# Forms of the input made in place and in smaller steps, weight splits of one stretch at a higher priority, sums of weights behind their low parts, and a buffer moved by 32 bytes

## The chip, the core and the metric

The kernel runs on one core of a Trainium2 chip. The core has five engines with queues of their own: PE (TensorE, matmuls), DVE (VectorE), ACT (ScalarE), POOL (GpSimd) and SP (SyncE, which here only issues transfers). They share an on-chip memory of 128 partitions; matmuls add into a smaller memory, PSUM. The metric is the device time of one execution in microseconds (us), lower is better. Of the kernel before three runs are shown, of which the median counts.

## What is computed

One layer of a decoder on 256 rows of 2048 numbers, float32. Cut to the projections around the change:

```python
h = rms_norm(x, ln1_g[l])
proj = h @ w_in[l]
aq, ak, av, iq, ik, iw, rq, rk, rv, rg, ga, gb = jnp.split(proj, offsets, axis=-1)
o_attn = dsa_attention(...)                    # top-k of an indexer, 16 heads
y_ret = retention_chunkwise(rq, rk, rv, log_gamma)
o_ret = jax.nn.silu(rg) * group_norm_heads(y_ret, ...)
merged = jax.nn.sigmoid(ga) * (o_attn @ w_up_attn[l]) + jax.nn.sigmoid(gb) * (o_ret @ w_up_ret[l])
x = x + merged @ w_out[l]
x = x + jnp.square(jax.nn.relu(rms_norm(x, ln2_g[l]) @ w_ff1[l])) @ w_ff2[l]
```

The change touches the projections `ga` and `gb` (the gates, 2048 columns each) and what is made for them.

## The kernel before

**One product.** Every large product is made of three fp32r matmuls. A float32 number is split into a high part, rounded to fp32r, and a low part, the rest. `split` (L337) does this for 128x1024 weights at a time: ACT copies them to fp32r (`whi`, L350), and DVE subtracts that from the raw weights (`wlo`, L351). `products` (L397) then issues, for each 128x512 of weights and each activation, high times high (L401), high activation times low weight (L402) and low activation times high weight (L403). The weights are the moving operand, the activations are the stationary one. `whi` and `wlo` have three buffers each. Raw weights of 128x2048 float32 (1 MB) arrive by SP's queue into one of three places: a ring of four, a pair of buffers `rawb` in the pool `cx`, or the two halves of `rawc`. Loads are asked for up to eight items ahead of their use, splits two items ahead (`ahead`, L360).

**The woven stretch.** The four gate units GA0, GA1, GB0 and GB1 (1024 columns each) are made in seven products instead of eight half-size ones, as in Strassen's scheme. Four of the seven have a weight quarter plus another one, or a form of the input, a difference of two of its quarters, as a factor. A unit has 28 items Q0 to Q27 of 6 matmuls, four for each product. They are woven with 80 items of 12 matmuls of other projections: RV2 and RV3, UA0 to UA3, RQ0 and RQ1, RK0 and RK1, eight items each (RV2.0 is the first of RV2). The order is written by `gates` (L132): Q0, RV2.0, Q1, RV2.1, Q2, RV2.2, Q3, Q4, RV2.3, Q5, RV2.4, Q6, Q7 and so on. `strassen` (L640) makes an item Q; behind the last item of each product it copies the result out (ACT) or adds it into results that stand on chip (DVE, L657), and where a quarter of the result is finished, `gate` applies the sigmoid (ACT, L462) and sends it to memory (POOL). These results and copies are called `stg`.

**Sums of weights.** Quarter A plus B, B plus C, C plus A and D plus C are made by DVE at L343, on 128x2048 elements in place in the raw buffer of the first. The table `SUMS` (L119) says ahead of which item each is made; `split` issues it just before that item's high part.

**Forms of the input.** G5, G6, G3 and G7 are kept as high and low parts in `hx` (4 forms of 128x1024 each, twice). Before the first gate, between the blocks RV0 and RV1, two tiles `xr` are loaded with the transposed input (L738). They take the two `rawb` buffers, into which weights go afterwards. `h_forms` (L698) runs as a generator beside the matmuls of RV1, one step at a time, each step between two pieces of the block: ACT multiplies `xr` by the gains (L704, 16 instructions of 128x256, two steps of eight), then for each form DVE subtracts (L710, 128x1024, into a tile `tmp`), ACT copies the high part (L711) and DVE subtracts the low part (L712). `tmp` has the tag `big2` with a single buffer, and `rawc` follows in the same buffer; so no load into `rawc` can start before `tmp` is done with. RV2's weights, the first of the woven stretch to use `rawc`, come that way.

**What sets the order.** All code is written as one stream of instructions, and a scheduler orders each engine's part by priority, which follows the place in the stream, and by when operands are expected. On the chip each engine then works strictly in that order.

## Time and profile before

| What | Value |
|---|---|
| Time, median of 3 runs | 1642.29 us (1640.89 to 1643.23) |
| The profiled execution's own time | 1642.31 us |
| Its span, first to last instruction | 1640.5 us |
| Mean granted TensorE clock | 0.997 |
| Woven stretch | from about 272 us to 670 us |
| Load of `xr`, issue to landing | 6.4 us |

The profile takes its times from one execution. A row of the timeline has the start in us from the span's start, the duration in us, the engine, the line, the operation, out<-in with the tiles' names, the shape and a count of equal instructions in a row; in brackets the idle time before it and what ended that. Matmuls are pipelined: a row lasts about 0.39 us, and the next one starts after 0.23 us. In the table of windows each engine has its busy time and the number of its instructions in the stretch, and PEclk is the mean granted clock. A row of the tile view has minimum, median and maximum of the durations in ns and the first and last start in us. A wait row has total us, times and longest us.

### The profile page before, as it was taken

To read this page: it belongs to the slowest core of one execution; us is meant where nothing else is said; L and a number is where in the kernel's file an instruction comes from. 1 tells how busy PE (TensorE), PEld (TensorE's weight loads), DVE (VectorE), ACT (ScalarE), POOL (GpSimd) and SP (SyncE) were. 2 spreads that over 40 slices of the span, in tenths; PEclk is the share of its full clock that TensorE was granted. 3 is DMA by queue.
4 is the path that set the end of the run, shared out by engine and by line. 5 is a ranking of instruction groups with operands and counts; after the bars stand their busy time and mean duration, and the time that the engine had idled before them with its cause. 6 is when DMAs were issued, how large, how long until landed. Compare 5 with 4: busy or idle time off the path is not lost.

```text
span 1640.5 us, 19424 instructions
## 1 busy us (share of the span) xinstructions
PE 1622.0 (99%) x7366; PEld 1330.5 (81%) x7366; DVE 1268.3 (77%) x1307; ACT 1000.1 (61%) x1238; POOL 100.4 (6%) x141
## 2 busy tenths in 40 slices
PE   9999998999999999999999999999999999999998
PEld 8977886788878778888888878888888888888887
DVE  5577675878787898677665478898989898989874
ACT  7556566566565656544444576766767676767672
POOL 0000000000000000000110000000000000000000
PEclk9999999999999999999999999999999999999999
DMA  9634347465567645744777654767777777667583
GB/s 333 224 132 178 133 150 281 162 232 209 218 246 277 225 148 187 263 154 177 259 256 261 214 210 188 234 228 231 231 231 231 231 231 226 228 217 230 176 252 134
DMA packets 68206, 353.88 MB, mean 216 GB/s; under 512 B 7696, under 2 KB 14480, under 8 KB 31888
## 3 DMA queue, kind: packets, MB, share of 16 engines
q1 hardware_dynamic: 51616, 311.32, 51.3%
q0 software_dynamic: 13760, 35.14, 9.7%
q10 hardware_dynamic: 2736, 6.18, 1.0%
q8 instruction: 58, 0.95, 0.2%
q14 instruction: 36, 0.29, 0.0%
HBM read 325.34 MB, written 27.26 MB: 215 GB/s over the span
## 4 chain that ended last, share of the span: by engine, by line
PE 90%; DVE 5%; issue 2%; ACT 2%; DMA 1%; POOL 0%; DVEq 0%; SPq 0%; ACTq 0%; POOLq 0%
PE pm L402 14%; PE pm L403 14%; PE pm L401 13%; PE pq L402 8%; PE pq L403 8%; PE pq L401 8%; PE pf L401 7%; PE pf L403 7%; PE pf L402 7%; DVE wlo L351 2%; PE pt L430 1%; ACT whi L350 1%; PE pa L628 1%; PE pa L601 1%; DVE raw L343 1%
## 5 line engine op out<-in xcount | busy, mean ns | idle before, releaser
L351 DVE TENSOR_TENSOR wlo<-raw,whi 128x1024 fp32r<-128x1024 f32 (+2 forms) x528 | 626.9, 1199 | 243.0 <-ACT whi L350 236.9
L350 ACT ACTIVATE whi<-raw 128x1024 fp32r<-128x1024 f32 (+2 forms) x528 | 546.3, 1041 | 405.2 <-PE pm L403 270.7
L402 PE MATMUL pm<-wlo,act 128*128 128x512 f32 (+1 forms) x1056 | 409.7, 388 | 8.6 <-DVE wlo L351 8.6
L401 PE MATMUL pm<-whi,act 128*128 128x512 f32 (+1 forms) x1056 | 414.7, 397 | 1.8 <-ACT whi L350 1.8
L403 PE MATMUL pm<-whi,act 128*128 128x512 f32 (+1 forms) x1056 | 408.3, 387 | 0.0
L351 DVE TENSOR_TENSOR wlo<-rawc,whi 128x1024 fp32r<-128x1024 f32 x192 | 234.2, 1220 | 59.1 <-ACT whi L350 57.4
L350 ACT ACTIVATE whi<-rawc 128x1024 fp32r<-128x1024 f32 x192 | 203.4, 1059 | 102.8 <-PE pm L403 44.2
L402 PEld LDWEIGHTS pm<-wlo,act 128*128 128x128 f32 x1056 | 199.1, 189 | 53.0 <-DVE wlo L351 15.3
L401 PEld LDWEIGHTS pm<-whi,act 128*128 128x128 f32 x1056 | 198.6, 188 | 43.7 <-ACT whi L350 4.0
L403 PEld LDWEIGHTS pm<-whi,act 128*128 128x128 f32 x1056 | 199.0, 188 | 38.0
L343 DVE TENSOR_TENSOR raw<-raw,raw 128x2048 f32<-128x2048 f32 x88 | 201.1, 2285 | 0.8
L401 PE MATMUL pf<-whi,act 128*128 128x512 f32 x512 | 200.1, 391 | 0.0
L402 PE MATMUL pf<-wlo,act 128*128 128x512 f32 x512 | 199.4, 389 | 0.0
L403 PE MATMUL pf<-whi,act 128*128 128x512 f32 x512 | 199.4, 389 | 0.0
L401 PE MATMUL pq<-whi,xf 128*128 128x512 f32 x392 | 154.4, 394 | 0.0
L403 PE MATMUL pq<-whi,xf 128*128 128x512 f32 x392 | 152.8, 390 | 0.0
L402 PE MATMUL pq<-wlo,xf 128*128 128x512 f32 x392 | 152.6, 389 | 0.0
L401 PEld LDWEIGHTS pf<-whi,act 128*128 128x128 f32 x512 | 96.1, 188 | 20.1 <-ACT whi L350 0.4
L403 PEld LDWEIGHTS pf<-whi,act 128*128 128x128 f32 x512 | 96.1, 188 | 20.1
L402 PEld LDWEIGHTS pf<-wlo,act 128*128 128x128 f32 x512 | 96.2, 188 | 19.8
L403 PEld LDWEIGHTS pq<-whi,xf 128*128 128x128 f32 x392 | 73.6, 188 | 15.4
L402 PEld LDWEIGHTS pq<-wlo,xf 128*128 128x128 f32 x392 | 73.7, 188 | 14.7
(167 smaller groups left out, 1416.4 us busy)
## 6 DMA issues: line engine op xcount, KB each, us to landing
raw<-in_w_dram SPq DMA_DIRECT2D x180, 1024.0 KB, 5.8
rawc<-in_w_dram SPq DMA_DIRECT2D x96, 1024.0 KB, 5.8
sums<-ev POOLq DMA_DIRECT2D x56, 256.0 KB, 5.5
raw<-in_w_dram SPq DMA_DIRECT2D x8, 736.0 KB, 4.7
raw<-in_w_dram SPq DMA_DIRECT2D x7, 512.0 KB, 7.3
raw<-in_w_dram SPq DMA_DIRECT2D x8, 368.0 KB, 7.7
stg<-in_x_dram SPq DMA_DIRECT2D x8, 256.0 KB, 7.6
rv<-stg POOLq DMA_DIRECT2D x8, 256.0 KB, 4.3
```

What stands on the lines that cost most here:

```text
L343: nc.vector.tensor_tensor(one, one, two, op=ALU.add)
L350: nc.scalar.activation(a, src, AF.Copy)
L351: nc.vector.tensor_tensor(b, src, a.bitcast(F32), op=ALU.subtract)
L401: nc.tensor.matmul(d, h, hi, start=first, stop=False, skip_group_check=skip)
L402: nc.tensor.matmul(d, h, lo, start=False, stop=False, skip_group_check=skip)
L403: nc.tensor.matmul(d, l, hi, start=False, stop=last, skip_group_check=skip)
L430: nc.tensor.transpose(ps[:, c * P:(c + 1) * P], src[:, c * P:(c + 1) * P], ident)
L601: nc.tensor.matmul(ps[:, a * n:(a + 1) * n], qT[:, h0 + a, :], kT[:, j, :n], start=True, stop=True)
L628: nc.tensor.matmul(po, vv[:, c, j * HD:(j + 1) * HD], pT, start=(c == 0), stop=(c == t))
```

## The change

It has five parts.

1. **Sums behind low parts.** A table of its own, `GATE_SUMS`, holds for the gate units; five of its eight places are one or two items earlier than in `SUMS`. For the gates the sum is issued behind the low part of its item instead of ahead of the high part.
2. **Priority of splits.** From 16 items before the first gate item to the last one, `split` runs at a priority raised by 60 places.
3. **Forms in place and paced.** There is no `tmp` any more: each difference overwrites a quarter of `xr` that is not needed again. The forms come in the order G5, G7, G6, G3. The scaling goes in 8 steps of two instructions instead of two steps of eight, and there is a step between each high and low part.
4. **`rawc` early.** Without `tmp`, `rawc` takes its buffer directly after the load of `xr` is issued.
5. **One more small buffer.** `n_sm` goes from 24 to 25, 32 bytes more in each partition. The buffers allocated behind it move; `hx` goes from byte 113888 of its partition to 113856, from 32 to 0 modulo 64, and `xr`, `rawc`, `stg` and some smaller tiles also come to a multiple of 64. `act`, `xf`, `whi` and `wlo` stand at multiples of 64 before and after.

```diff
+GATE_SUMS = {2: ("A", "B", 0), 5: ("A", "B", 1), 9: ("B", "C", 0), 11: ("B", "C", 1),
+             14: ("C", "A", 0), 16: ("C", "A", 1), 22: ("D", "C", 0), 24: ("D", "C", 1)}
...
-    n_stg, n_mid, n_sm = 8, 11, 24
+    n_stg, n_mid, n_sm = 8, 11, 25
...
-            one = SUMS.get(4 * item[2] + 2 * item[3] + item[4])
+            one = (GATE_SUMS if item[1] in GATES else SUMS).get(4 * item[2] + 2 * item[3] + item[4])
...
+    first_gate = use.index(("Q", GATES[0], 0, 0, 0))
+    last_gate = len(use) - 1 - use[::-1].index(("Q", GATES[-1], len(ORDER) - 1, HK // KC - 1, HT - 1))
+
     def split(i):
+        if first_gate - 16 <= i <= last_gate:
+            with tc.high_priority(offset=AHEAD):
+                split_now(i)
+        else:
+            split_now(i)
+
+    def split_now(i):
...
-        if sum_of(item):
+        early = sum_of(item) and item[1] not in GATES
+
+        def total():
             one, two = (raws[z] for z in sum_of(item))
             nc.vector.tensor_tensor(one, one, two, op=ALU.add)
+
+        if early:
+            total()
...
             nc.scalar.activation(a, src, AF.Copy)
             nc.vector.tensor_tensor(b, src, a.bitcast(F32), op=ALU.subtract)
+        if sum_of(item) and not early:
+            total()
...
     def h_forms(raw):
 
-        tmp = px.tile([P, 4, HK, P], F32, tag="big2", name="tmp")
         for k in range(HK):
             for j in range(2):
                 z, g = raw[j][:, k, :], g1[:, j * HK + k:j * HK + k + 1]
                 nc.scalar.activation(z, z, AF.Copy, scale=g)
-            if k % 4 == 3:
-                yield
+            yield
         (x11, x21), (x12, x22) = ([raw[j][:, :, t * P:(t + 1) * P] for t in range(T)] for j in range(2))
-        for i, (f, one, two) in enumerate(((G5, x21, x22), (G6, x11, tmp[:, 0]), (G3, x12, tmp[:, 1]), (G7, x21, x11))):
-            d, hi, lo = tmp[:, i], hx[:, 0, f - G5], hx[:, 1, f - G5]
+        for f, d, one, two in ((G5, x22, x21, x22), (G7, x21, x21, x11), (G6, x11, x11, x22), (G3, x12, x12, x11)):
+            hi, lo = hx[:, 0, f - G5], hx[:, 1, f - G5]
             nc.vector.tensor_tensor(d, one, two, op=ALU.subtract)
             nc.scalar.activation(hi, d, AF.Copy)
+            yield
             nc.vector.tensor_tensor(lo, d, hi.bitcast(F32), op=ALU.subtract)
-            yield
-        late["rawc"] = px.tile([P, 2, KC, BN], F32, tag="big2", name="rawc")
+            if f != G3:
+                yield
...
+            late["rawc"] = px.tile([P, 2, KC, BN], F32, tag="big2", name="rawc")
             work.append(h_forms(raw))
```

The number of instructions of each kind stays the same. Behind the woven stretch the order of the engines stays the same too, but for two matmuls of the attention that change places.

How the order moves at the places of which the prediction speaks. First DVE at the end of RV1, before the change. Rows with `raw_387`, `raw_394` and `raw_409` are RV1's own low parts; `xr_427` and `xr_428` are the two halves of the input.

```order
L351 TENSOR_TENSOR wlo_437_2336<-raw_394_2110,whi_436_2335 128x1024
L710 TENSOR_TENSOR tmp_2284<-xr_427_2272 128x1024
L710 TENSOR_TENSOR tmp_2284<-xr_427_2272,xr_428_2273 128x1024
L351 TENSOR_TENSOR wlo_439_2358<-raw_394_2110,whi_438_2357 128x1024
L710 TENSOR_TENSOR tmp_2284<-xr_427_2272,tmp_2284 128x1024
L712 TENSOR_TENSOR hx_2271<-tmp_2284,hx_2271 128x1024
L710 TENSOR_TENSOR tmp_2284<-xr_428_2273,tmp_2284 128x1024
L712 TENSOR_TENSOR hx_2271<-tmp_2284,hx_2271 128x1024 x3
L351 TENSOR_TENSOR wlo_442_2378<-raw_409_2185,whi_441_2377 128x1024
L351 TENSOR_TENSOR wlo_444_2395<-raw_409_2185,whi_443_2394 128x1024
```

The same place after the change; here `wlo_447` is the low part of Q0 of GA0, and `wlo_449` that of RV2.0.

```order
L368 TENSOR_TENSOR wlo_437_2323<-raw_394_2110,whi_436_2322 128x1024
L368 TENSOR_TENSOR wlo_439_2343<-raw_394_2110,whi_438_2342 128x1024
L368 TENSOR_TENSOR wlo_443_2367<-raw_409_2185,whi_442_2366 128x1024
L368 TENSOR_TENSOR wlo_445_2387<-raw_409_2185,whi_444_2386 128x1024
L727 TENSOR_TENSOR xr_428_2273<-xr_427_2272,xr_428_2273 128x8x128
L727 TENSOR_TENSOR xr_427_2272<-xr_427_2272 128x8x128
L368 TENSOR_TENSOR wlo_447_2406<-raw_431_2279,whi_446_2405 128x1024
L730 TENSOR_TENSOR hx_2271<-xr_428_2273,hx_2271 128x1024
L368 TENSOR_TENSOR wlo_449_2425<-rawc_2276,whi_448_2424 128x1024
L730 TENSOR_TENSOR hx_2271<-xr_427_2272,hx_2271 128x1024
```

Before, all eight instructions of the forms (four differences, four low parts) stood ahead of RV1's last two low parts. Now all of RV1's low parts stand ahead of the first form, and of the forms only two differences stand ahead of Q0's low part. ACT moves likewise: before, its 16 scalings stand in one piece between two high parts of RV1, and after they stand in pieces of five, four, five and two with a high part between.

Second, DVE in the first unit, GA0, after the change, from the low part of RV2.2 (`wlo_463`) to that of Q6 (`wlo_478`); Q3 is `wlo_465`, Q4 `wlo_467`, RV2.3 `wlo_470`, Q5 `wlo_473`, RV2.4 `wlo_476`.

```order
L368 TENSOR_TENSOR wlo_463_2493<-rawc_2276,whi_462_2492 128x1024
L730 TENSOR_TENSOR hx_2271<-xr_427_2272,hx_2271 128x1024
L368 TENSOR_TENSOR wlo_465_2509<-raw_440_2362,whi_464_2508 128x1024
L727 TENSOR_TENSOR xr_428_2273<-xr_428_2273,xr_427_2272 128x8x128
L368 TENSOR_TENSOR wlo_467_2519<-raw_431_2279,whi_466_2518 128x1024
L368 TENSOR_TENSOR wlo_470_2537<-rawc_2276,whi_469_2536 128x1024
L730 TENSOR_TENSOR hx_2271<-xr_428_2273,hx_2271 128x1024
L368 TENSOR_TENSOR wlo_473_2550<-raw_431_2279,whi_472_2549 128x1024
L357 TENSOR_TENSOR raw_440_2362<-raw_440_2362,raw_455_2460 128x2048
L368 TENSOR_TENSOR wlo_476_2562<-rawc_2276,whi_475_2561 128x1024
L357 TENSOR_TENSOR raw_441_2364<-raw_441_2364,raw_468_2534 128x2048
L368 TENSOR_TENSOR wlo_478_2578<-raw_440_2362,whi_477_2577 128x1024
```

Before, there were the same low parts and three sums in this piece, and nothing of the forms: the sums stood ahead of Q3, of RV2.3 and of Q6, and a fourth ahead of Q2. Now low parts of two forms and one difference stand among them, and the sums stand behind the low parts of Q2 (just ahead of this piece), Q5 and RV2.4.

Third, DVE at the end of the unit GA0. Before, `wlo_539` is the low part of Q21, `wlo_541` that of RV3.7 and `wlo_543` that of Q22; the rows of L657 are the additions behind Q19.

```order
L351 TENSOR_TENSOR wlo_539_2926<-raw_521_2822,whi_538_2925 128x1024
L657 TENSOR_TENSOR stg_520_2820<-stg_537_2916,stg_520_2820 128x512
L657 TENSOR_TENSOR stg_486_2627<-stg_537_2916,stg_486_2627 128x512
L657 TENSOR_TENSOR stg_520_2820<-pq_474_2554,stg_520_2820 128x512
L351 TENSOR_TENSOR wlo_541_2942<-rawc_2361,whi_540_2941 128x1024
L343 TENSOR_TENSOR raw_521_2822<-raw_521_2822,raw_468_2535 128x2048
L351 TENSOR_TENSOR wlo_543_2954<-raw_528_2867,whi_542_2953 128x1024
```

After the change:

```order
L368 TENSOR_TENSOR wlo_539_2925<-raw_521_2822,whi_538_2924 128x1024
L676 TENSOR_TENSOR stg_520_2820<-stg_537_2915,stg_520_2820 128x512
L357 TENSOR_TENSOR raw_521_2822<-raw_521_2822,raw_468_2534 128x2048
L368 TENSOR_TENSOR wlo_541_2941<-rawc_2276,whi_540_2940 128x1024
L368 TENSOR_TENSOR wlo_543_2952<-raw_528_2866,whi_542_2951 128x1024
L368 TENSOR_TENSOR wlo_545_2963<-rawc_2276,whi_544_2962 128x1024
L676 TENSOR_TENSOR stg_520_2820<-pq_474_2554,stg_520_2820 128x512
L676 TENSOR_TENSOR stg_486_2626<-stg_537_2915,stg_486_2626 128x512
```

The sum now stands ahead of RV3.7's low part, and two of the additions stand behind the low parts of RV3.7, Q22 and the item after it.

More of the change, by code (lines that the diff above doesn't have):

```diff
@@ L300, in ring @@
         return key in BESIDE or (key[0] == "F2" and key[1] < NG - 1)
-    LOAD_AHEAD, SPLIT_AHEAD = 8, 2
+    LOAD_AHEAD, SPLIT_AHEAD, AHEAD = 8, 2, 60
     HT = KC // HC
```

## The prediction

> **What bounds the kernel now.** I read the page first, for the engine that sets the end.
>
> ```profile
> span 1640.5 us, 19424 instructions
> PE 1622.0 (99%) x7366; PEld 1330.5 (81%) x7366; DVE 1268.3 (77%) x1307; ACT 1000.1 (61%) x1238; POOL 100.4 (6%) x141
> ```
>
> PE works 99% of the span. The instructions stay the same in number and shape, so a gain can only come out of the 18.5 us in which PE idles, out of matmuls that run slower than others, and out of a lowered clock. The waits of PE, the second view, say what it idles for.
>
> ```profile
> PE pm L402 <- DVE wlo L351: 8.6, 9, 3.7
> PE pm L401 <- ACT whi L350: 1.8, 4, 0.5
> PE pq L402 <- DVE wlo L351: 0.8, 1, 0.8
> PE pq L401 <- ACT whi L350: 0.7, 1, 0.7
> ```
>
> Split weights account for 11.9 us: low parts from DVE for 9.4, high parts from ACT for 2.5. The third view is the table of windows over the woven stretch.
>
> ```profile
> core 0: us, PE busy (x) PEld busy (x) DVE busy (x) ACT busy (x) POOL busy (x), PEclk, DMA share, GB/s
> 249.00:264.36 15.36, 15.36 (x67) 11.85 (x65) 5.62 (x6) 11.00 (x23) 0.64 (x2) 1.00 0.79 289
> 264.36:284.00 19.64, 13.46 (x45) 9.48 (x43) 13.10 (x13) 9.17 (x11) 0.54 (x1) 0.83 0.78 315
> 284.00:298.00 14.00, 13.47 (x59) 10.82 (x59) 13.71 (x10) 8.32 (x10) 0.54 (x1) 1.00 0.33 122
> 298.00:320.00 22.00, 21.30 (x92) 16.80 (x91) 19.15 (x15) 11.94 (x12) 0.00 (x0) 1.00 0.35 124
> 320.00:415.00 95.00, 94.56 (x409) 76.16 (x409) 77.49 (x62) 59.09 (x62) 5.40 (x10) 1.00 0.61 227
> ```
>
> One stretch of 20 us is bad: from 264.36 PE idles 6.2 us, and its clock is granted at 0.83 on the mean. Just before it, DVE works 5.62 of 15.36 us; just behind it, 13.71 of 14.00. DVE's work is badly placed there, not too much: from 320 on it is busy 82% and PE 99.5%. The timelines show why. First PE:
>
> ```profile
> 254.84 0.39 PE L403 MATMUL pm<-whi,act 128*128 128x512 f32 x1
> ...
> 264.36 0.39 PE L403 MATMUL pm<-whi,act 128*128 128x512 f32 x1
> ...
> 275.21 0.80 PE L402 MATMUL pm<-wlo,act 128*128 128x512 f32 x1 [3.66 <-DVE wlo L351]
> ...
> 276.23 0.63 PE L402 MATMUL pm<-wlo,act 128*128 128x512 f32 x1
> ...
> 283.99 0.73 PE L401 MATMUL pm<-whi,act 128*128 128x512 f32 x2
> ...
> 285.25 0.50 PE L402 MATMUL pm<-wlo,act 128*128 128x512 f32 x1 [0.53 <-DVE wlo L351]
> ...
> 300.19 0.50 PE L402 MATMUL pm<-wlo,act 128*128 128x512 f32 x1 [0.69 <-DVE wlo L351]
> ```
>
> Then DVE and ACT in the same time:
>
> ```profile
> 268.26 1.22 DVE L712 TENSOR_TENSOR hx<-tmp,hx 128x1024 fp32r<-128x1024 f32 x1
> 269.40 1.22 DVE L710 TENSOR_TENSOR tmp<-xr,tmp 128x1024 f32<-128x1024 f32 x1
> 270.53 3.49 DVE L712 TENSOR_TENSOR hx<-tmp,hx 128x1024 fp32r<-128x1024 f32 x3
> 273.94 3.49 DVE L351 TENSOR_TENSOR wlo<-raw,whi 128x1024 fp32r<-128x1024 f32 x3
> ...
> 287.77 2.28 DVE L343 TENSOR_TENSOR raw<-raw,raw 128x2048 f32<-128x2048 f32 x1
> 289.97 1.22 DVE L351 TENSOR_TENSOR wlo<-raw,whi 128x1024 fp32r<-128x1024 f32 x1
> ```
>
> ```profile
> 257.59 6.49 ACT L704 ACTIVATE xr<-xr,gT 128x256 f32<-128x256 f32 x16
> 263.99 1.05 ACT L350 ACTIVATE whi<-raw 128x1024 fp32r<-128x1024 f32 x1
> ```
>
> ACT scales `xr` for 6.49 us in one piece, and RV1's next high part waits until 263.99. The forms then run in one piece on DVE, and RV1's last two low parts start behind them, at 273.94. PE waits 3.66 us, and the matmuls behind that wait take 0.63 to 0.80 us instead of 0.39: a lowered clock.
>
> **The change part by part.** The price of a matmul: the rows at 254.84 and 264.36 stand 42 matmuls apart by the program, so 9.52 / 42 = 0.2267 us each. Of DVE: a low part or a difference 1.14 us in a row (3.49 for three, the last with its 1.22), a sum 2.20 (287.77 to 289.97).
>
> *The forms' place.* Between 264.36 and 283.99 lie 43 steps by the program. Fed all the time, they take 43 x 0.2267 = 9.75, so the row of 283.99 would start at 274.11. The loss is 9.9 us, waits and lowered clock together. Afterwards DVE has all of RV1's low parts ahead of the first form, and the 5.62 busy of 15.36 us say that it has time for them. ACT's scalings come in pieces of at most five, 5 x 0.41 = 2.0 us, within one item of 12 matmuls (2.72 us), and PE has splits for two items. So the whole 9.9 goes. What is late next is Q0's low part, behind two differences; it has 1.14 x 2 + 1.22 = 3.5 us to go after RV1's last low part, which stands two items ahead of PE, so it is in time. If that cover is gone (`xr` lands late, say), half of the wait of 3.66 comes back.
>
> *The stops behind it.* The wait at 285.25 is that of RV2.0's low part, still in DVE's heap; I cost it at 1.0 with the restart (0.53 of idle, and the row of 0.50 instead of 0.39 with its neighbours). The one at 300.19, with a sum ahead of the low part, at 0.69 plus as much for its restart as there, in all 1.1. Both come from DVE's backlog and go: -2.1.
>
> *The new backlog.* Six of the eight instructions of the forms (four low parts, two differences) now stand among the splits of GA0's first items, that is 6 x 1.14 = 6.8 us of DVE in a place where it worked 13.71 of 14.00. Let t0 be the start of Q0. The buffer for Q1's high part comes free at t0; 1.05 for it, Q1's low part 1.14, a difference 1.14 and RV2.1's low part 1.22 give t0 + 4.55, with hand-offs about 4.9 (an estimate). From there to the end of Q6's low part stand three sums, ten instructions of 1.14 and the last with 1.22: 6.6 + 11.4 + 1.2 = 19.2, so t0 + 24.1. PE wants it at t0 + 22.0: the items ahead of Q6 have 96 matmuls, 21.8, and the first L402 comes one later. That is 2.1 late; with a restart I take **+2.2**. Bounds: 0, if the hand-offs are shorter and DVE starts Q1 earlier (its low parts may run ahead while buffers last), and 4, if `hx`'s high parts on ACT also delay the splits.
>
> *Sums behind low parts, priority.* In the other three units DVE's order of sums and low parts up to Q19 is as before, by the built program. At a unit's end the sum now stands ahead of RV3.7's low part (+2.20) and two additions less do.
>
> ```profile
> 448.86 1.28 DVE L657 TENSOR_TENSOR stg<-stg,stg 128x512 f32<-128x512 f32 x2
> ```
>
> An addition is 0.64. So that low part comes 2.20 - 2 x 0.64 = 0.9 later, and Q22's earlier by 1.3. Before, PE idles little there (0.44 us in all of 320 to 415). Net between -3 and +3 over four units; I take **+0.5**, nearer to nothing because the row of 320 to 415 leaves so little to win.
>
> *The address of `hx`.* The tile view of the gates' PSUM tiles separates matmuls with `hx` from those with `act`:
>
> ```profile
> L401 PE MATMUL pq<-whi,hx x128: 392/394/496, 297.2 to 641.0; 128*128 128x512 f32 x128
> L402 PE MATMUL pq<-wlo,hx x128: 388/399/400, 297.4 to 641.2; 128*128 128x512 f32 x128
> L403 PE MATMUL pq<-whi,hx x128: 390/392/399, 297.7 to 641.4; 128*128 128x512 f32 x128
> L401 PE MATMUL pq<-whi,act x96: 387/389/494, 271.1 to 669.0; 128*128 128x512 f32 x96
> L402 PE MATMUL pq<-wlo,act x96: 389/389/504, 282.8 to 669.3; 128*128 128x512 f32 x96
> L403 PE MATMUL pq<-whi,act x96: 387/389/476, 283.0 to 669.5; 128*128 128x512 f32 x96
> ```
>
> Medians are 5, 10 and 3 ns longer with `hx`, which starts at 32 modulo 64; `act` starts at 0. If the address is the cause, 128 x 18 ns = 2.3 us go. Against it speak two rows of plain float32, where `mid` stands at 32 modulo 64 and `rqk` at 0:
>
> ```profile
> L620 PE MATMUL pt<-csb,mid 128*128 128x128 f32 x48 | 7.2, 272 | 0.0
> ...
> L800 PE MATMUL pa<-rqk 128*128 128x128 f32 x16 | 3.1, 274 | 0.0
> ```
>
> There the address makes no difference; but those are other matmuls. I take **-2.3** (between -2.3 and 0), since within the gates nothing else distinguishes the two tiles. A rule speaks against it: the Trainium skill, "TensorE: Matmul & The Clock Gate", section "Step-by-step: what each phase is for", has two independent read ports, one for the stationary operand, and the load's time goes by columns alone. By that the term would be 0, and the sum 2.3 higher; "SBUF — State Buffer", section "Operand start alignment", asks for a multiple of the element's size only and says that this is about legality and not speed.
>
> *`rawc` early, transfers.* The first row is of SP's timeline, the second of the page's list of transfers:
>
> ```profile
> 274.05 0.80 SPq L321 DMA_DIRECT2D rawc<-in_w_dram  x2
> ```
>
> ```profile
> rawc<-in_w_dram SPq DMA_DIRECT2D x96, 1024.0 KB, 5.8
> ```
>
> `rawc`'s first loads start at 274.05, when `tmp` is done with; they are needed about 10 us later, now some 10 us earlier. Issued directly behind `xr`, they are there in time (5.8 us). But `xr`'s two buffers are now read until the low parts of G6 and G3, about t0 + 10.5 and t0 + 16.1 in the ledger above, and two weight tiles wait for them on SP, with other loads behind. They are needed at t0 + 20 and later; 5.8 us of landing after 10.5 and 16.1 gives 16.3 and 21.9. Hidden, at nothing, but with little to spare.
>
> Sum: -9.9 - 2.1 + 2.2 + 0.5 - 2.3 = -11.6. The profiled execution took 1642.31, its span 1640.5 and 1.8 outside; the median of the three runs is 1642.29, so nothing is to be corrected: **1630.7**.
>
> **The rivals.** *The address does nothing* (the two rows of plain float32 for it, the tile view against it): 1633.0. By the rule of the Trainium skill named above this would be the outcome.
>
> *No new backlog*: DVE runs ahead of PE in RV1 and keeps that. For it: DVE is 63% idle in RV1. Against it: three buffers allow it no lead beyond two items. Without +2.2 and +0.5: 1628.0.
>
> *DVE becomes the bound in each unit*: the sums behind low parts delay the next item in GA1, GB0 and GB1 too as I have it in GA0, 3 x 2.2 = 6.6: 1637.3. Against it: there DVE is busy 82%, and nothing of the forms is left.
>
> *Slower: SP's queue blocks.* If the two weight tiles that wait for `xr`'s buffers stand ahead of loads that PE needs soon, PE stops for a landing, 5.8, and the clock falls as at 275, where the window's 0.83 over 19.64 us stands for 0.17 x 19.64 = 3.3. Two such stops, each 5.8 + 3.3 = 9.1, give 18.2: 1648.9. It decides once `xr` is released 4 us later than in my ledger. Against it: the loads are asked for eight items ahead.
>
> **How the numbers follow.** Forecast 55%, address without effect 20%, no backlog 14%, DVE bound 7%, slower 4%. The likeliest case's own range is 1627.5 to 1633 (its terms for the backlog, 0 to 4, and the ends of units). The range of all is 1625.5 to 1636: its lower end is the second rival with 2.5 off at the units' ends, its upper end the first with the ends of units at +3. It leaves out the last two rivals. A measurement of this kernel can tell about 0.2%, 3.3 us, from no change: faster means below 1639.0, slower above 1645.6. Faster is all but the slower rival and a margin of 2%: 0.94; within 0.2%, 0.02; slower 0.04.
>
> **What would show it.** In the profile after: no lowered clock and no wait over 1 us between 255 and 285; Q0 starting about 10 us earlier against the same matmul count; DVE busy nearly all the time between 282 and 297, with short waits of L402 about 20 to 24 us behind Q0's start (the backlog); medians of L401 to L403 with `hx` at 389 (the address). Long waits on a DMA between 275 and 300 would show the slower rival, waits of half a microsecond to two at the same places of GA1, GB0 and GB1 the one of DVE. I am wrong if a wait with a lowered clock stands anywhere in the stretch.

## The result, and the profile after

| | median, us | runs | span of the profiled execution | clock |
|---|---|---|---|---|
| before | 1642.76 | 1640.89 to 1643.65 (4) | 1640.5 | 0.997 |
| after | 1630.58 | 1630.22 to 1630.73 (4) | 1629.0 | 1.0 |

The ratio is 0.9927, with a 95% interval of 0.991 to 0.9944: faster by 12.2 us in the medians and 11.5 in the spans. The forecast was 1630.7. Two single executions at a much lower granted clock (2719.60 us with 24 small buffers, 1785.65 in the run on the ends) are left out of the medians below. The page of the kernel after:

```profile
span 1629.0 us, 19406 instructions
PE 1616.6 (99%) x7366; PEld 1330.7 (82%) x7366; DVE 1268.6 (78%) x1307; ACT 1000.1 (61%) x1238; POOL 100.4 (6%) x141
```

DVE, ACT and POOL work as long as before. PE idles 12.4 us instead of 18.5. Its waits now (L420 to L422 are the lines L401 to L403 of before, L367 and L368 those of the high and the low part):

```profile
PE pm L420 <- ACT whi L367: 2.4, 5, 0.5
PE pm L421 <- DVE wlo L368: 2.0, 5, 0.6
...
PE pq L420 <- ACT whi L367: 1.2, 2, 0.9
PE pq L421 <- DVE wlo L368: 0.5, 1, 0.5
```

The waits for split weights fell from 11.9 to 6.1 us, and the longest from 3.7 to 0.9. By stages:

```profile
core 0: us, PE busy (x) PEld busy (x) DVE busy (x) ACT busy (x) POOL busy (x), PEclk, DMA share, GB/s
...
264.36:284.00 19.64, 19.64 (x88) 16.07 (x87) 17.88 (x16) 15.27 (x19) 1.08 (x2) 1.00 0.62 234
284.00:298.00 14.00, 12.56 (x54) 9.66 (x53) 14.00 (x11) 7.46 (x8) 0.00 (x0) 1.00 0.56 225
```

From 264.36 to 284 PE has no gap, 88 matmuls instead of 45, at full clock. The next 14 us, where DVE does not rest at all, have become the bad ones, 1.4 us of idle PE. The two waits in them:

```profile
272.98 0.39 PE L420 MATMUL pq<-whi,act 128*128 128x512 f32 x1
...
293.81 0.50 PE L420 MATMUL pq<-whi,hx 128*128 128x512 f32 x1 [0.93 <-ACT whi L367]
...
297.11 0.50 PE L421 MATMUL pq<-wlo,hx 128*128 128x512 f32 x1 [0.52 <-DVE wlo L368]
```

And DVE at that time:

```profile
290.30 2.28 DVE L357 TENSOR_TENSOR raw<-raw,raw 128x2048 f32<-128x2048 f32 x1
292.50 1.22 DVE L368 TENSOR_TENSOR wlo<-rawc,whi 128x1024 fp32r<-128x1024 f32 x1
293.64 2.28 DVE L357 TENSOR_TENSOR raw<-raw,raw 128x2048 f32<-128x2048 f32 x1
295.84 2.35 DVE L368 TENSOR_TENSOR wlo<-raw,whi 128x1024 fp32r<-128x1024 f32 x2
```

Q0 starts at 272.98. Q6's low part ends at 295.84 + 1.22 = 297.06, that is 24.1 behind Q0, and PE waits for it. It waits once more just ahead, for Q6's high part: ACT can only make that once the sum of 290.30 is done. No lowered clock and no wait over 0.93 us stands in the woven stretch, which is what the prediction named as its sign of being wrong.

Both traces hold 7366 matmuls in nearly the same order, so the start of the same matmul, by its number, can be compared. Where the order differs, a number stands for a neighbouring matmul in the other trace, which is worth about 0.23 us a place. This is the running account of the gain:

| matmul number, place | before, us | after, us | difference, us |
|---|---|---|---|
| 36, start of the kernel | 8.49 | 8.70 | +0.2 |
| 1344, in Q0 | 283.00 | 273.43 | -9.6 |
| 1416, in RV2.3, ahead of Q6 | 301.45 | 289.95 | -11.5 |
| 1440, in Q6, behind its waits | 306.98 | 297.44 | -9.5 |
| 2532, end of GB0 | 560.75 | 552.83 | -7.9 |
| 2724, in GB1 | 606.71 | 595.71 | -11.0 |
| 2928, near the end of GB1 | 653.51 | 642.31 | -11.2 |
| 3780, much later | 839.71 | 828.28 | -11.4 |

So there are three gains (9.8, 1.9 and 3.1) and two losses (2.0 and 1.6).

### The profile page after: what moved, and what is told of

It is laid out like the page before. It is cut to its first block, busy times and chain, and to the rows that moved or that the text cites. A ratio compares the mean times of both kernels' runs of the same rounds, so it can differ in the third digit from the quotient of the medians.

```text
span 1629.0 us, 19406 instructions
## 1 busy us (share of the span) xinstructions
PE 1616.6 (99%) x7366; PEld 1330.7 (82%) x7366; DVE 1268.6 (78%) x1307; ACT 1000.1 (61%) x1238; POOL 100.4 (6%) x141
## 4 chain that ended last, share of the span: by engine, by line
PE 92%; DVE 4%; ACT 2%; issue 1%; DMA 0%; POOL 0%; DVEq 0%; POOLq 0%; ACTq 0%
PE pm L421 14%; PE pm L422 14%; PE pm L420 14%; PE pq L421 8%; PE pq L422 8%; PE pq L420 8%; PE pf L420 7%; PE pf L422 7%; PE pf L421 7%; DVE wlo L368 2%; PE pt L449 1%; ACT whi L367 1%; DVE raw L357 1%; PE pa L647 1%; PE pa L620 1%
## 5 line engine op out<-in xcount | busy, mean ns | idle before, releaser
L368 DVE TENSOR_TENSOR wlo<-raw,whi 128x1024 fp32r<-128x1024 f32 (+2 forms) x528 | 627.5, 1200 | 244.9 <-ACT whi L367 238.5
L367 ACT ACTIVATE whi<-raw 128x1024 fp32r<-128x1024 f32 (+2 forms) x528 | 546.9, 1042 | 403.1 <-PE pm L422 262.7
L420 PE MATMUL pm<-whi,act 128*128 128x512 f32 (+1 forms) x1056 | 414.4, 395 | 2.4 <-ACT whi L367 2.4
L421 PE MATMUL pm<-wlo,act 128*128 128x512 f32 (+1 forms) x1056 | 407.3, 386 | 2.0 <-DVE wlo L368 2.0
L422 PE MATMUL pm<-whi,act 128*128 128x512 f32 (+1 forms) x1056 | 407.3, 386 | 0.0
L368 DVE TENSOR_TENSOR wlo<-rawc,whi 128x1024 fp32r<-128x1024 f32 x192 | 234.5, 1221 | 50.9 <-ACT whi L367 49.3
L367 ACT ACTIVATE whi<-rawc 128x1024 fp32r<-128x1024 f32 x192 | 203.5, 1060 | 103.1 <-PE pm L422 44.4
L421 PEld LDWEIGHTS pm<-wlo,act 128*128 128x128 f32 x1056 | 198.5, 188 | 43.6 <-DVE wlo L368 6.1
L420 PEld LDWEIGHTS pm<-whi,act 128*128 128x128 f32 x1056 | 198.4, 188 | 43.4 <-ACT whi L367 4.6
L422 PEld LDWEIGHTS pm<-whi,act 128*128 128x128 f32 x1056 | 198.3, 188 | 37.7
L420 PE MATMUL pf<-whi,act 128*128 128x512 f32 x512 | 200.0, 391 | 0.0
L421 PE MATMUL pf<-wlo,act 128*128 128x512 f32 x512 | 199.4, 389 | 0.0
L422 PE MATMUL pf<-whi,act 128*128 128x512 f32 x512 | 199.4, 389 | 0.0
L420 PE MATMUL pq<-whi,xf 128*128 128x512 f32 x392 | 154.3, 394 | 0.0
L422 PE MATMUL pq<-whi,xf 128*128 128x512 f32 x392 | 152.7, 390 | 0.0
L421 PE MATMUL pq<-wlo,xf 128*128 128x512 f32 x392 | 152.6, 389 | 0.0
L422 PEld LDWEIGHTS pf<-whi,act 128*128 128x128 f32 x512 | 96.1, 188 | 20.1
L420 PEld LDWEIGHTS pf<-whi,act 128*128 128x128 f32 x512 | 96.0, 188 | 20.0 <-ACT whi L367 0.4
L421 PEld LDWEIGHTS pf<-wlo,act 128*128 128x128 f32 x512 | 96.2, 188 | 19.8
L422 PEld LDWEIGHTS pq<-whi,xf 128*128 128x128 f32 x392 | 73.6, 188 | 15.5
L421 PEld LDWEIGHTS pq<-wlo,xf 128*128 128x128 f32 x392 | 73.7, 188 | 14.7
```

The costliest lines, as they stand in the source:

```text
L367: nc.scalar.activation(a, src, AF.Copy)
L368: nc.vector.tensor_tensor(b, src, a.bitcast(F32), op=ALU.subtract)
L420: nc.tensor.matmul(d, h, hi, start=first, stop=False, skip_group_check=skip)
L421: nc.tensor.matmul(d, h, lo, start=False, stop=False, skip_group_check=skip)
L422: nc.tensor.matmul(d, l, hi, start=False, stop=last, skip_group_check=skip)
```

## The experiments

The differences "by number" below are made as in the table above, against the kernel after or before, in one profiled execution each. Two places differ from trace to trace without a cause in the edits: the start of the kernel (by up to 1.0 us at matmul 36) and the surroundings of matmul 3768 (by up to 1.9); what is read off lies between them. Ratios are to the kernel before on the same chip.

**The forms alone.** The kernel before with the new `h_forms` and `rawc` allocated ahead of it:

```diff
             for j, z in enumerate(raw):
                 nc.sync.dma_start(z, xt[:, j * HK:(j + 1) * HK, :])
+            late["rawc"] = px.tile([P, 2, KC, BN], F32, tag="big2", name="rawc")
             work.append(h_forms(raw))
```

> The kernel before with the forms in place and paced and rawc early, and nothing else of the change (sums, priority and address as before). My theory: the loss of 9.9 us at 264 to 284 goes, because the forms no longer stand ahead of RV1's low parts and rawc's loads no longer wait for tmp. But without the priority DVE makes seven of the eight form instructions ahead of RV2.0's low part and the last ahead of Q2's; by the ledger from the rows of the changed kernel (Q0 at 273.0, 1.14 a low part, 2.20 a sum) Q1's low part comes 0.6 late, Q4's about 1.7 more and Q6's about 1.1 more: 3.4 of waits between Q0 and Q6 where the changed kernel has 2.0. With the ends of units and the address as before: about 1634 us. Rival: the priority does the work, and without it the forms still stop PE near Q0 for over 3 us with a lowered clock: 1638 or more.

Measured: 1635.14 us, ratio 0.9956 (0.9941 to 0.9971). The forms alone bring 7.4 of the 12.2 us. No wait near Q0 is over 0.6 us:

```profile
276.29 0.50 PE L402 MATMUL pm<-wlo,act 128*128 128x512 f32 x1 [0.60 <-DVE wlo L351]
...
279.70 0.50 PE L402 MATMUL pq<-wlo,act 128*128 128x512 f32 x1 [0.17 <-DVE wlo L351]
...
290.91 0.50 PE L402 MATMUL pq<-wlo,hx 128*128 128x512 f32 x1 [1.18 <-DVE wlo L351]
...
299.86 0.50 PE L402 MATMUL pq<-wlo,hx 128*128 128x512 f32 x1 [0.50 <-DVE wlo L351]
```

The rival, that the priority keeps PE fed there, falls. The waits in GA0 are 2.5 us, at RV2.0, Q1, Q4 and Q6, of which the ledger had the last three; by number, with restarts and small delays, this kernel loses 2.0 more from Q0 to Q6 than the kernel after, so 4.0 where that one has 2.0. The ledger had 3.4.

**The forms back.** The kernel after with `h_forms`, `tmp` and the late `rawc` of before; priority, sums and address stay.

```diff
+        tmp = px.tile([P, 4, HK, P], F32, tag="big2", name="tmp")
...
+        late["rawc"] = px.tile([P, 2, KC, BN], F32, tag="big2", name="rawc")
...
-            late["rawc"] = px.tile([P, 2, KC, BN], F32, tag="big2", name="rawc")
```

> The changed kernel with the forms as before (tmp, two steps of eight scalings, rawc behind tmp), and with the priority, the sums and the address of the change. My theory: the priority alone saves little, since rawc's first loads still wait until the last low part of the forms has read tmp. DVE now does RV1's low parts first, the last form's low part ends at about 276, the load lands 5.8 later, and the high and the low part take 2.3 more: RV2.0's low part comes at about 284, 9 us later than PE could use it (275), and the clock falls: no wait for RV1's low parts, but one of 8 to 10 us at RV2.0; about 1642 us, as the kernel before, within 2. Rival: what cost 9.9 was the forms ahead of RV1's low parts, the priority removes it, and rawc early is worth nothing: 1631 to 1633.

Measured: 1644.11 us, ratio 1.0011 (1.0002 to 1.0021), no faster than before. RV1's low parts are in time now, and PE stops once, at RV2.0. The chain of that stop is in four timelines, of DVE, SP, ACT and PE:

```profile
276.07 2.36 DVE L731 TENSOR_TENSOR hx<-tmp,hx 128x1024 fp32r<-128x1024 f32 x2
```

```profile
278.46 12.50 SPq L323 DMA_DIRECT2D rawc<-in_w_dram  x3
```

```profile
286.02 1.06 ACT L367 ACTIVATE whi<-rawc 128x1024 fp32r<-128x1024 f32 x1 [8.85 <-DMA rawc<-in_w_dram]
```

```profile
287.13 1.22 PE L420 MATMUL pm<-whi,act 128*128 128x512 f32 x2 [12.81 <-ACT whi L367]
```

The last low part has read `tmp` at 278.43; the load is issued at 278.46; ACT, which waits for its landing, starts 7.6 later; the high part takes 1.06; PE has waited 12.81 us, longer than the 8 to 10 that I expected, and the granted clock is 0.72 on the mean from 284 to 298. So the transfer into `rawc` has to start early, which the forms without `tmp` make possible; without that, priority, sums and address together are worth nothing. The other half, `rawc` early with the forms still ahead of RV1's low parts, was not run.

**No priority.** The kernel after, with `split_now(i)` called without `tc.high_priority`.

> The changed kernel without the raised priority of the splits; all else as changed. My theory: the forms stand ahead of RV2.0's and Q1's low parts now, but the ledger gives waits of about 0.6 at Q1, 0.9 at RV2.2 and 0.2 at RV2.3 in place of those at Q6, about 2 in all as before. The additions of a unit's end stand ahead of RV3.7's low part again, as in the kernel before, which gives back what the ends of units and the rotations near 597 gained (about 1.0): 1631.5 us. Rival: the priority is what keeps PE fed at the forms: a wait over 3 us near Q0, 1636 or more.

Measured: 1633.26 us, ratio 0.9951 (0.9934 to 0.9968). The rival falls here too: the waits in GA0 are chiefly one of 0.60 at RV2.0 and one of 1.04 at Q4, not at the places that I gave, but small. By number this kernel is 1.0 behind the one after when Q6 is done, then gains 2.0 up to matmul 2532, at the ends of GA0, GA1 and GB0, and loses 3.3 from there to 2724. That last piece I had counted too low. In all the priority is worth 2.0 us in the spans. DVE at that last piece, without priority:

```profile
547.02 1.09 DVE L706 TENSOR_TENSOR rot<-stg,rtab 128x256 f32<-128x256 f32 x3
548.02 0.68 DVE L708 TENSOR_TENSOR stg<-stg,rot 128x512 f32<-128x512 f32 x1
548.62 0.42 DVE L706 TENSOR_TENSOR rot<-stg,rtab 128x256 f32<-128x256 f32 x1
...
550.70 2.29 DVE L356 TENSOR_TENSOR raw<-raw,raw 128x2048 f32<-128x2048 f32 x1
552.90 1.22 DVE L367 TENSOR_TENSOR wlo<-raw,whi 128x1024 fp32r<-128x1024 f32 x1
```

And the kernel after:

```profile
545.95 2.28 DVE L357 TENSOR_TENSOR raw<-raw,raw 128x2048 f32<-128x2048 f32 x1
548.15 2.35 DVE L368 TENSOR_TENSOR wlo<-raw,whi 128x1024 fp32r<-128x1024 f32 x2
...
553.90 0.69 DVE L709 TENSOR_TENSOR stg<-stg,rot 128x512 f32<-128x512 f32 x1
554.50 0.76 DVE L707 TENSOR_TENSOR rot<-stg,rtab 128x256 f32<-128x256 f32 x2
555.17 1.22 DVE L368 TENSOR_TENSOR wlo<-rawc,whi 128x1024 fp32r<-128x1024 f32 x1
```

The rotations of RQ and RK (`rotated`) stood in a block, and behind them the sum of 550.70 and the low part of 552.90. With the priority, the sum (545.95) and low parts stand ahead of the rotations and between their pieces. Without it PE waits at 554.17, for the low part of 552.90:

```profile
554.17 0.51 PE L420 MATMUL pq<-wlo,act 128*128 128x512 f32 x1 [1.06 <-DVE wlo L367]
```

**Sums back.** The kernel after with the table `SUMS` for the gates as well, each sum issued ahead of its high part. (Six of the eight places of `GATE_SUMS` are earlier than in `SUMS`, not five as said above.)

> The changed kernel with the sums of the gates where they were in code (table SUMS, ahead of the high part), with the priority and all else as changed. By the built order only one sum of the first piece moves: it stands behind RV2.4's low part now instead of ahead, so Q6's high part comes 1.1 later and RV2.4's low part 2.2 earlier. My theory: the sums' place is worth little beside the priority, Q6's low part comes at the same time: between 1630.2 and 1631.2 us. Rival: the sum behind the low part is what makes the ends of units shorter: waits of up to 1 us more at each unit's end, 1633 or more.

Measured: 1631.68 us, ratio 0.9932 (0.9917 to 0.9947). By number it is 0.4 behind at the start of the kernel and also when the woven stretch ends, so the sums' place is worth nothing within that stretch. In GA0 the two waits are replaced by one of 1.39 near 297. The waits at the units' ends are those of the kernel after, so the priority makes them and not the sums' place. What the time has more than expected, lies behind the stretch (0.6 near matmul 3768, 0.25 in small pieces after it), where nothing was changed.

**The address, undone, alone, and further.** `n_sm` 24 in the kernel after, 25 in the kernel before, 27 in the kernel after.

> The changed kernel with 24 small buffers as before, so that hx starts at 32 modulo 64 again; nothing else changes. From the steps of the two traces: from L402 to L403 with hx 237 ns before, 232 after, the other two steps 231 to 232 in both. My theory: the address is worth 128 x 5 ns = 0.65 us, no more, so about 1631.2, and the median of L403's predecessor in the tile view goes back to 399 ns. Rival one, as I predicted it: 2.3, so 1632.9. Rival two: the address does nothing and the 5 ns come from elsewhere (order, DMA): 1630.6, and the tile view stays at 393.

> The kernel before with 25 small buffers, so that hx starts at a multiple of 64, and nothing else of the change. My theory: 0.65 us less than before, which is hardly to be told from none in the time, but the median of L402 with hx goes from 399 to about 393 ns. Rival: 2.3 us less, with all three medians at 389 as with act.

> The changed kernel with 27 small buffers: hx starts at byte 113792 of its partition, a multiple of 128, where it is 64 modulo 128 in the changed kernel. With hx a matmul still takes 232 ns from start to start there, with act and xf 227. My theory: act and xf stand at 64 modulo 128 too and run at 227, so a multiple of 128 changes nothing: 1630.6, steps of 232. Rival: the rest of 5 ns is a matter of alignment as well and goes: 384 x 5 ns = 1.9, so 1628.7, steps of 227.

Measured: 1631.62 us, ratio 0.993 (0.9917 to 0.9944); 1641.69, ratio 0.9994 (0.9985 to 1.0003); 1630.83, ratio 0.9927 (0.9914 to 0.9939). The times don't tell them apart, the tile views do. First the kernel after:

```profile
L420 PE MATMUL pq<-whi,hx x128: 390/394/500, 286.7 to 629.8; 128*128 128x512 f32 x128
...
L421 PE MATMUL pq<-wlo,hx x128: 390/393/497, 287.2 to 630.0; 128*128 128x512 f32 x128
...
L422 PE MATMUL pq<-whi,hx x128: 389/395/404, 287.4 to 630.2; 128*128 128x512 f32 x128
```

With 24 small buffers in it:

```profile
L420 PE MATMUL pq<-whi,hx x128: 392/394/494, 287.4 to 631.0; 128*128 128x512 f32 x128
...
L421 PE MATMUL pq<-wlo,hx x128: 392/399/499, 287.8 to 631.2; 128*128 128x512 f32 x128
...
L422 PE MATMUL pq<-whi,hx x128: 388/392/399, 288.1 to 631.4; 128*128 128x512 f32 x128
```

With 27:

```profile
L420 PE MATMUL pq<-whi,hx x128: 392/398/501, 287.4 to 630.4; 128*128 128x512 f32 x128
...
L421 PE MATMUL pq<-wlo,hx x128: 388/396/502, 287.8 to 630.6; 128*128 128x512 f32 x128
...
L422 PE MATMUL pq<-whi,hx x128: 392/396/401, 288.1 to 630.9; 128*128 128x512 f32 x128
```

Going back to 32 modulo 64 brings the 399 back, and the address alone takes it from 399 to 393 in the kernel before. So the address does something. How much, the medians don't tell: from 32 to 0 modulo 64 the 399 falls by 6, but the median of L422 rises from 392 to 395. The steps from the start of one matmul with `hx` to the next show more (means in ns, without the few steps over 300 behind a wait):

| `hx` starts at | kernels | L420 to L421 | L421 to L422 | L422 to L420 | sum |
|---|---|---|---|---|---|
| 32 modulo 64 | before, forms alone, 24 buffers in after | 231.7 to 232.3 | 236.0 to 236.5 | 231.6 to 231.7 | 699.8 to 699.9 |
| 64 modulo 128 | after, 25 buffers in before, the eight other runs with 25 | 234.2 to 234.6 | 232.4 to 232.9 | 231.1 to 231.4 | 697.9 to 698.6 |
| 0 modulo 128 | 27 buffers in after | 233.4 | 233.3 | 234.2 | 701.0 |

One step becomes 4 ns shorter and the one before it 2 to 3 longer, as nearly a third of these now take 240. Together that is 1.6 ns for three steps, 128 x 1.6 = 0.2 us. By number the address is worth more, 0.6 in the kernel after and 0.5 in the kernel before from matmul 1344 to 2928; what is beyond 0.2 lies in matmuls without `hx`, and as `xr`, `rawc` and `stg` move too, no run tells which tile makes it. A multiple of 128 is no better. With `act` the three steps take 227 each by the median; most of the difference to `hx`, about 5 ns a step, stays at every address tried, and its cause is open.

**Low parts twice.** This kernel makes two low parts of the forms a second time, with the same result.

```diff
             nc.vector.tensor_tensor(lo, d, hi.bitcast(F32), op=ALU.subtract)
+            if f in (G6, G3):
+                nc.vector.tensor_tensor(lo, d, hi.bitcast(F32), op=ALU.subtract)
```

> The changed kernel in which the low parts of the forms G6 and G3 are each made twice, the second time with the same result: 2 x 1.14 = 2.3 us more of DVE between the low part of RV2.2 and that of Q5. My theory: in GA0 DVE is the bound from RV2.1 to Q6, so all of it is added to the waits at Q6's parts: 2.0 becomes about 4.3, 1632.9 us. Rival: there is slack, the waits near 294 and 297 come from something else (the sum behind Q5, a transfer): under 1 us more, 1631.5 or less.

Measured: 1634.12 us, ratio 0.9946 (0.9933 to 0.996). By number it is 0.6 behind the kernel after at the start and 2.9 behind at Q6, so 2.3 from the added 2.3: DVE bounds that piece without slack. The clock stays at 1.00 behind the wait of 2.36 (the window from 290 to 300).

```profile
288.77 0.50 PE L421 MATMUL pq<-wlo,hx 128*128 128x512 f32 x1 [0.60 <-DVE wlo L368]
...
296.69 0.50 PE L420 MATMUL pq<-whi,hx 128*128 128x512 f32 x1 [2.36 <-ACT whi L367]
```

**Low parts on POOL.** The same two low parts, on POOL instead of DVE.

```diff
-            nc.vector.tensor_tensor(lo, d, hi.bitcast(F32), op=ALU.subtract)
+            (nc.vector if f in (G5, G7) else nc.gpsimd).tensor_tensor(lo, d, hi.bitcast(F32), op=ALU.subtract)
```

> The changed kernel with the low parts of the forms G6 and G3 made by POOL (GpSimd) instead of DVE. DVE has 2 x 1.14 = 2.3 us less in the piece where it is the bound, from RV2.1 to Q6; the run with these two made twice came 2.3 later there. My theory: the waits near 294 and 297 in GA0, 1.9 with their restarts, nearly all go: 1628.7 us. Rival: DVE's own instructions become slower while POOL works, or POOL takes so long that the buffers of xr, and the weights loaded into them, come late: no gain, 1630.5 or more.

Measured: 1637.94 us, ratio 0.9977 (0.9968 to 0.9986), 7 us slower than the change. My theory failed, and the rival held, by its second branch. POOL (each low part by itself), SP, DVE and PE in turn:

```profile
277.89 15.71 POOL L730 TENSOR_TENSOR hx<-xr,hx 128x1024 fp32r<-128x1024 f32 x1 [2.36 <-ACT hx L728]
...
293.56 2.39 POOL L730 TENSOR_TENSOR hx<-xr,hx 128x1024 fp32r<-128x1024 f32 x1
```

```profile
293.63 2.68 SPq L323 DMA_DIRECT2D raw<-in_w_dram  x2
296.40 0.38 SPq L323 DMA_DIRECT2D rawc<-in_w_dram  x1
```

```profile
290.12 1.21 DVE L368 TENSOR_TENSOR wlo<-rawc,whi 128x1024 fp32r<-128x1024 f32 x1
298.44 2.29 DVE L357 TENSOR_TENSOR raw<-raw,raw 128x2048 f32<-128x2048 f32 x1 [7.11 <-DMA raw<-in_w_dram]
```

```profile
301.92 0.80 PE L421 MATMUL pq<-wlo,hx 128*128 128x512 f32 x1 [6.10 <-DVE wlo L368]
302.51 0.63 PE L422 MATMUL pq<-whi,hx 128*128 128x512 f32 x1
```

POOL takes 15.71 us for the first low part and 2.39 for the second; DVE takes 1.14 in a row. What differs is what DVE does meanwhile. It works without a pause until 290.12 + 1.21 = 291.33, on instructions with two operands in the on-chip memory, and POOL's first low part ends 2.27 later, at 293.60. The second one runs while DVE stands idle. So POOL is kept out as long as DVE works, and DVE only stops when it runs out of weights. The buffers of `xr` come free late, the loads into them are issued from 293.63 on (285.91 in the kernel after), and DVE waits 7.11 us for the weights. This is the mechanism of the prediction's slower rival: `xr` released late. The wait near 294 is gone here: at matmul 1428 this kernel is 0.7 ahead of the one after.

The Trainium skill, "SBUF — State Buffer", section "Who interferes with whom", says that a DVE instruction with two inputs from the on-chip memory contends with a POOL instruction that reads there. The trace agrees, with 15.71 us beside a busy DVE and 2.39 beside an idle one; DVE loses nothing by it and keeps its 1.21 us.

**Ends.** The kernel after without priority for six splits behind Q19 in three units:

```diff
+    ends = {use.index(("Q", u, 4, HK // KC - 1, HT - 1)) + j for u in GATES[:3] for j in range(3, 9)}
...
-        if first_gate - 16 <= i <= last_gate:
+        if first_gate - 16 <= i <= last_gate and i not in ends:
```

> The changed kernel with the priority taken away from six splits at the end of each of the units GA0, GA1 and GB0 (the third to eighth item behind Q19), so that the additions behind Q19 stand ahead of RV3.7's low part again, and the sum behind it. Measured without any priority, these ends were 0.5, 1.0 and 0.9 us shorter, but the stretch from 553 to 596, with the rotations, 3.3 longer. My theory: the additions' place decides at the ends and the priority elsewhere decides for the rotations, so the ends give about 1 to 1.5 us (GB0's end lies among the rotations and may give nothing): 1629.3 us. Rival: the two hang together, since a split held back at an end is behind for the next unit's first items: no gain, 1630.6 or more.

Measured: 1631.64 us, ratio 0.9936 (0.9923 to 0.995). By number against the kernel after it gains 1.5 up to the end of GA1, another 0.7 at GB0's first wait, and loses 1.8 between matmuls 2484 and 2544, at GB0's end, where the rotations stand; another 1.0 is lost near matmul 3768, behind the stretch, where nothing was changed. Inconclusive as a time, clear as an account: at GA0 and GA1 the priority costs, at GB0 it pays.

> Both of the edits before in one kernel: two low parts of the forms on POOL, no priority for six splits at the end of three units. My theory: they lie in different places and add up: 1.9 and about 1.2 less than the changed kernel, 1627.5 us. Rival: what one gives the next unit's first items take back: 1628.7 or more.

With the low parts on POOL as well: 1637.58 us, ratio 0.9971 (0.996 to 0.9981); it stops as the run with POOL alone does, with the same two durations on POOL (15.71 and 2.39), and says nothing further of the ends.

**Another version.** The exception for GA0 and GA1 only (`GATES[:2]`), and a quarter of the scaling on DVE:

```diff
-                nc.scalar.activation(z, z, AF.Copy, scale=g)
+                if j and k % 2:
+                    nc.vector.tensor_scalar(z, z, g, None, op0=ALU.mult)
+                else:
+                    nc.scalar.activation(z, z, AF.Copy, scale=g)
```

> The changed kernel with two edits that lie in different places. First, four of the sixteen scalings of the input are made by DVE, in its idle time between RV1's low parts, so ACT is done with the scaling earlier and the first form starts about 1.7 us earlier on DVE, which has worked without a pause from there to 301. My theory: the backlog at Q6 falls by that, but a sum now stands ahead of RV2.3's low part, which by the ledger comes 1.0 late; so the 1.9 of waits in GA0 become about 1.0. Second, the priority is taken from the six splits at the end of GA0 and GA1 alone, and not at GB0, where the run before lost between 550 and 553 what it had gained: -1.5 at these two ends, and GB0 as in the changed kernel. Together 1630.6 - 0.9 - 1.5 = 1628.2 us. Rival: what is gained at GA1's end is taken back at GB0's, or DVE's scalings are so slow that RV1's low parts come late: 1630.5 or more.

Measured: 1629.24 us, ratio 0.9917 (0.9904 to 0.9931), span 1627.5. By number, against the kernel after, the two ends give 1.65, as expected, and GB0 takes nothing back. The backlog in GA0 gives 0.25 at most. The first form starts at 264.27 instead of 267.53, but the sum ahead of RV2.3's low part makes the wait that the expectation named, and a second one stands at RV2.5, behind the sum after that:

```profile
289.51 0.50 PE L423 MATMUL pm<-wlo,act 128*128 128x512 f32 x1 [1.03 <-DVE wlo L370]
...
299.60 0.50 PE L423 MATMUL pm<-wlo,act 128*128 128x512 f32 x1 [0.34 <-DVE wlo L370]
```

It is the fastest of the kernels here by its median. Its interval overlaps that of the change, so that it beats the change is shown by the accounts, not by the times.

## Why the prediction was right, and where it was not

*The forms' place, -9.9.* Measured -9.8 by number, with no gap and full clock up to 284. The mechanism held, but not as I ranked its parts. I named the forms ahead of RV1's low parts as the cause and gave the early `rawc` one paragraph at nothing. The run with the forms back shows that RV1's low parts in time are worth nothing while RV2.0's weights wait for `tmp`. That the change takes away both at once kept the term right; as to `rawc`, that was luck. Whether `rawc` early would do alone, no run shows; against it stands the wait of 3.66 for RV1's low part in the trace before.

*The stops behind it, -2.1.* Measured -1.9. For the wait at 285.25 the amount is right and the cause is not. I put it down to DVE's heap, but DVE stood idle ahead of RV2.0's low part. It waited for the high part, which stood on ACT behind an eviction, and ACT was idle until PE's last matmul of RV1 released that (DVE, then ACT, in the kernel before):

```profile
283.97 1.23 DVE L351 TENSOR_TENSOR wlo<-rawc,whi 128x1024 fp32r<-128x1024 f32 x1 [6.54 <-ACT whi L350]
```

```profile
282.30 0.69 ACT L462 ACTIVATE stg<-pm,r 128x512 f32<-128x512 f32 x1 [10.35 <-PE pm L403]
282.88 1.05 ACT L350 ACTIVATE whi<-rawc 128x1024 fp32r<-128x1024 f32 x1
```

*The new backlog, +2.2.* Measured +2.0, Q6's low part at Q0 + 24.1 as worked out. The run with two low parts made twice added 2.3 for 2.3. What I did not see is that Q6's high part waits too, for the sum that the change puts behind Q5's low part.

*The ends, +0.5.* This term failed. Within it are +1.6 to +2.1 (the ends of GA0, GA1 and GB0, depending on how much of the address's gain is counted there) and -3.1 (the end of GB0 and the first items of GB1). The first I had within my bounds. The second is no end of a unit but the rotations with a sum behind them, of which the prediction does not speak: it weighed the priority by sums and additions alone. The run without priority loses them again (3.3).

*The address, -2.3.* Mis-sized: about -0.6 by number, of which 0.2 is shown in the steps with `hx`. The claim that nothing else distinguishes `hx` from `act` was wrong, since about 5 ns a step stay at three addresses; the medians of 389 that I had named as the sign did not come (394, 393 and 395). The rule of the Trainium skill, "TensorE: Matmul & The Clock Gate", section "Step-by-step: what each phase is for", by which the term is 0, is nearer to the measurement, but not exact: the sum of the three steps moves by 1.6 ns with the address alone.

So the sum of -11.6 against -11.5 in the spans is better than its terms, and that is luck. The two wrong ones, +0.5 and -2.3, sum to -1.8; in their place stand about -1.1 and -0.6. The slower rival did not occur, as DVE releases `xr` early: with POOL in its place it came, for about 7 us and not 9.1 for one stop.

## What to carry to other kernels

Before crediting a gain to an order on one engine, follow the next transfer: here the buffer of a temporary held up a load, and a better order alone was worth nothing. A change of priorities acts wherever anything competes, so list all work that stands in the stretch, not only what the change names. Compare two traces by the number of the instruction on the bound engine; the steps of that difference show gains and losses that a total hides. A merged row and a median hide things too: two POOL instructions of 18.07 us together took 15.71 and 2.39, and a median that fell by 6 ns stood for steps that sum to 1.6 less.

## What the runs showed of the hardware

- A float32 subtraction of 128x1024 took POOL 15.71 us while DVE ran subtractions and sums without a pause, and ended 2.27 us after DVE's last; the next one, with DVE idle, took 2.39 (both runs with low parts on POOL). DVE does one in 1.22 and was not slowed.
- The step from one matmul to the next depended a little on where its stationary operand `hx` starts. By the median one step of three took 232 ns at a multiple of 64 bytes and 237 at 32 modulo 64, but by the mean another grew, and the three together differed by 1.6 ns. With `act` and `xf` a step took 227.
- A wait of 2.36 us (low parts twice) left the granted clock at 1.00. The waits of 3.66 (before), 6.10 (low parts on POOL) and 12.81 us (forms back) were followed by matmuls of 0.63 to 0.80 us instead of 0.39. No run has one between 2.36 and 3.66.
